# A planner's port model and durations: how a recording layer orders and places the instructions of a hybrid decoder layer

## The chip, the core and the metric

The kernel runs on one core of a Trainium2 chip. The metric is the device time of one execution in microseconds. Five engines work side by side, each through its own list of instructions in the order in which they were issued: TensorE (PE; its weight loads are shown as PEld), VectorE (DVE), ScalarE (ACT), GpSimd (POOL) and SyncE (SP, which here only starts DMAs). They wait for each other through semaphores. Matmuls write PSUM; the working memory is SBUF.

## What is computed

One layer of a hybrid decoder trunk in float32: 512 tokens of width 1024, 256 memory tokens, 4 heads in each of three groups, a feed-forward width of 2816. Cut to what matters:

```python
h = rmsnorm(x, norm_mix)
mem_h = rmsnorm(mem, norm_mem)
c_q, c_kv, k_rope, hq, hf, hi, hg, mq = split(h @ w_in)
y_mla = mla_group(c_q, c_kv, k_rope, ...)      # causal softmax attention, low-rank q and kv, rotary key
y_hg  = hgrn2_group(hq, hf, hi, hg, ...)       # gated linear recurrence
y_mem = mem_group(mq, mem_h, ...)              # softmax attention to 256 memory tokens
mix = concatenate([rmsnorm(y_mla), y_hg, rmsnorm(y_mem)])
x = x + mix @ w_out
h2 = rmsnorm(x, norm_ffn)
x = x + (silu(h2 @ w_gate) * (h2 @ w_up)) @ w_down
```

## The kernel before

**Products.** Every float32 operand of a large product is split into a high part, rounded to the matmul's type, and the rest: `split` makes `hi` on ACT (`A.copy`, or a scaled activation) and `lo = src - hi` on DVE, a `tensor_tensor` with two SBUF operands where the source is a weight. `mm3` then issues three matmuls for one product: hi x hi, hi x lo, lo x hi. In the trace the weights' parts are `wh` and `wl`, loaded into `wr` (or `mx` and `y` in the gate and up products); the activations' are `xh` and `xl`, `hd`, `v`, `mv`, `mx`, `pth` and `ptl`. PSUM tiles are `mm` (3 banks), `at` (3) and `tr` (2).

**Stages, in the order of the program:** x is split and its norm taken; HGRN2 with its levels (`hg_levels`, `hg_out`); the low-rank projections; rotary embedding (`rope`, on `qr` and `kr`) and causal attention by heads (`transposed`, `rope_t`, `softmax`, `weights_t`, `pv`), whose key transposes are `tr<-cst,tc`; attention to the memory; the output projection in two parts. The first part (blocks `OUT_ORDER[0:8]`) needs the first two groups and serves as filler beside the attention chains; the second (loop over `X_ORDER`) needs `group_norm` of the memory group: column sums, an inverse root in eleven small DVE instructions, four transposes `tr<-cst,sm` that spread it, then for each of four blocks a scaling on DVE, `xh` on ACT and `xl` on DVE. Behind each of the second part's eight blocks DVE adds the residual (`tm<-mm,tm`), scales (`y<-tm,RX`) and sums squares (`tc<-tc,tc`). Sums and differences of those blocks (tiles `p`, `td`) and their parts (`hd`, `v`, `mv`) are the left operands of the gate and up products: `fast` makes them by seven products instead of eight, in four rounds of columns (`FF`), with differences of weight blocks (`mx<-mx,mx`, `mx<-y,mx`) and of results. `down` (`mm` into `tr` or `mm`, `tr<-xh,wl` in the trace) is filled in between by `between`.

**What sets the order.** Nothing above is issued directly. `Recorder.record` (L102) takes down each call with its operands, its price (`price`, L183) and the other engines that can do the same (`others`, L160): an ACT copy can go to DVE; a DVE `tensor_tensor` on SBUF of at least 128 columns to POOL, with 500 ns added; a POOL `tensor_tensor` to DVE. `run` (L225) then plans: it keeps a time for each engine (`free`), for each instruction (`ready`, its predecessors' ends plus `LAT`) and for each buffer; again and again it takes, over all engines, the instruction that can start first, the more urgent one where two could start at once, and leaves an instruction to another engine where that would end it earlier. The result is one list in program order for each engine, and `issue` emits it. The engines on the chip keep each its own list's order, at their own speed. All instructions are thus issued from one line of the file, L350.

In the planner before, an engine is free when its own last instruction ends; what another engine does at that time doesn't matter. One price line of before, for POOL's `tensor_tensor`, and one for matmuls:

```python
return max(30 + 2.35 * m, 100 + 2.2 * m)
return (n * 0.417 + 3 if n >= 256 else 1.67 * n if n > 100 else 107) if ins[0].dtype == F32R else (1.676 * n if n > 100 else 214)
```

Of the kernel before, what the change touches and what calls it, by code (L numbers as in the profile page):

```python
# [20 lines left out]
NB = S // P  # L21
# [7 lines left out]
# columns of the packed vectors  # L29
# [16 lines left out]
class Recorder:  # L46
    """Takes down the instructions in program order, then issues them in an order
    that keeps the engines busy: by priority among those whose operands are there
    and whose buffers are free."""
# [20 lines left out]
    def last(self, eng):  # L70
        """the last instruction of an engine so far"""
        return next(o.n for o in reversed(self.ops) if o.eng == eng)

    @contextmanager
    def after(self, n):
        """keep back until an earlier instruction is through"""
        old, self.held = self.held, n
        yield
        self.held = old
# [22 lines left out]
    def record(self, eng, name, args, kw):  # L102
# [48 lines left out]
        o.alts = {eng: (name, args, kw, o.cost, 0)}  # L151
        for e, nm_, a, k in self.others(o, ins):
            q = _Op()
            q.eng, q.name, q.args, q.kw = e, nm_, a, k
            o.alts[e] = (nm_, a, k, self.price(q, outs, ins), {"gpsimd": 500}.get(e, self.MOVE if eng == "scalar" else 0))
# [4 lines left out]
    def others(self, o, ins):  # L160
        """other engines that do the same"""
# [20 lines left out]

    def price(self, o, outs, ins):  # L183
# [3 lines left out]
        if o.eng == "tensor":  # L187
            if o.name == "transpose":
                return 107
            if ins[0].dtype == F32 and self._free(ins[0]) <= 64 and n <= 64:  # L190
                return 65 if n <= 32 else 125
            return (n * 0.417 + 3 if n >= 256 else 1.67 * n if n > 100 else 107) if ins[0].dtype == F32R else (1.676 * n if n > 100 else 214)
        m = max([self._free(a) for a in ins] + [n])
        if o.eng == "scalar":
            fn = o.args[2] if o.name == "activation" else None
            if fn is not None:
                o.table = self.TABLES.get(str(fn).split(".")[-1])
            return 53 + 0.88 * m + (250 if "accum_out" in o.kw else 0) + (90 if hasattr(o.kw.get("scale"), "ap") else 0)
        if o.eng == "vector":
            if o.name == "reciprocal":  # L200
                return 70 + 6.6 * m
            fast = all(x.tensor.name not in self.tiles or self.tiles[x.tensor.name][4] == "SB" for x in ins)
# [13 lines left out]
        return max(30 + 2.35 * m, 100 + 2.2 * m)  # L216
# [8 lines left out]
    def run(self):  # L225
# [19 lines left out]
        table, dma, done, out = None, 0.0, 0, []  # L245
        busy = {e: 0.0 for e in engs}
        while done < len(ops):
            best = None
            for e in engs:
                be = None  # L250
                for o in cand[e]:
                    t = max(free[e], o.ready)
                    ok = True
# [20 lines left out]
                    if len(o.alts) > 1:  # L274
                        fin = t + o.alts[e][3] + o.alts[e][4]
                        late = False
                        for e2 in o.alts:
                            if e2 != e:
                                t2 = max(free[e2], o.ready)
                                if e2 == o.home or t2 + o.alts[e2][3] + o.alts[e2][4] < fin:  # L280
                                    back = sum(q.alts[e2][3] for q in cand[e2] if q.prio < o.prio and q.home == e2 and q.ready <= t2 + 200)
                                    if t2 + back + o.alts[e2][3] + o.alts[e2][4] < fin:
                                        late = True
# [15 lines left out]
            o.name, o.args, o.kw, cost, _ = o.alts[beste]  # L299
# [5 lines left out]
            end = t + cost  # L305
            free[o.eng] = end
# [67 lines left out]
def body(ctx, tc, t):  # L374
# [79 lines left out]
    def load(src, n=1024):  # L454
        """a [128, n] block of a weight"""
# [5 lines left out]
    def piece(raw, a, b):  # L461
        """some columns of a block, as their two parts"""
# [6 lines left out]
    def pieces(raw, n=1024):  # L469
        """k -> the k-th [128, 128] of a block, as its two parts"""  # L470
# [13 lines left out]
    def rsqrt_col(v, n):  # L484
        """v**-0.5 of a [128, n] block of positive numbers"""
# [9 lines left out]
    def colsum(sq, nblk):  # L495
        """column sums of [128, nblk*128], one per partition"""
# [5 lines left out]
    def spread(r):  # L502
        """[128, NB], by token, to [128, 512], the same on each partition"""
# [10 lines left out]
    def sumsq(srcs, acc=None, tag="td", eng=G):  # L514
        """elementwise sum of the squares of several [128, n] blocks"""
# [42 lines left out]
    def feat(dst, raw, acts):  # L558
        """dst [128 features, 512 tokens] from one block of columns"""
# [74 lines left out]
    def gated(i):  # L634
        """one block of the input projection, scaled by the norm of x"""
# [24 lines left out]
    def wide(src, n, banks, acts, use):  # L660
        """token-major products with one group of n columns"""
# [24 lines left out]
    def new_pt(ns):  # L686
        """transposed weights of two blocks of queries, keys on the partitions"""
        return sb("pth", (P, 8, P), F32R), sb("ptl", (P, 8, P), F32R)

    def pv(v, h, pt, ns, y):  # L690
        """y [128 values, 256 queries] of the products with ns blocks of keys"""
# [202 lines left out]
    # r * rsqrt(r^2 * mean + eps) by token and head  # L894
# [11 lines left out]
    def rope(src, nh):  # L906
        """rotate [128, NB, nh, 64] in place"""
# [51 lines left out]
    def transposed(src, h, scale=None):  # L959
        """one head of token-major blocks, by feature, as its two parts"""  # L960
# [8 lines left out]
    def softmax(src, nk, scale, neg, causal):  # L969
        """exp(scale * (src - max)) / sum by rows of a [128, nk] block of scores"""  # L970
# [12 lines left out]
    def weights_t(pp_, ns):  # L983
        """the softmax of two blocks of queries, transposed, as its two parts"""
# [8 lines left out]
    def group_norm(ys, i0, gname, tag):  # L993
        """RMS norm over four [128, 512] blocks, as operands of the output projection"""
# [8 lines left out]
    def rope_t(src, h):  # L1003
        """one head of [128, NB, 2, 64] blocks, by feature: their high parts and the source"""
# [115 lines left out]
    # a scale by token that keeps the tokens alike in size where sums of different ones are taken:  # L1120
    # about the norm so far; it goes out again with the norm
# [27 lines left out]
    # left operands of the seven products of the first layer, two blocks of inputs in each  # L1149
# [15 lines left out]
    def xsplit(src):  # L1165
        """two [128, 256] blocks, as the two parts"""
# [31 lines left out]
    def fast(src, c0, w, c):  # L1198
        """two groups of w columns, token-major, by the seven products of Winograd's form of
        Strassen's algorithm: over the halves of the tokens, of the inputs and of the columns"""  # L1200
# [63 lines left out]
    def between():  # L1264
        """a block of outputs of the second layer after every so many products"""
# [42 lines left out]
def pack(inp):  # L1308
    """the inputs as the program reads them: transposed and cut, values as they are"""
    c = np.ascontiguousarray  # L1310

    def kcut(w, cols):
        # [K, cols] -> [128, K/128 * cols]
# [73 lines left out]
```

## Time and profile before

| | us |
|---|---|
| device time, median of 3 runs | 799.17 (796.9 to 800.5) |
| span of the profiled execution, first to last instruction | 796.1 |
| mean granted TensorE clock in it | 0.980 |

The profile is of another execution than the three; only its span is known, and the median of the runs lies 3.1 us above it. A row of a group names the line, the engine, the operation, the tiles written and read (buffer numbers left out), the shape and the count; behind the bar the engine's busy time, the mean ns of one, then the idle time before these instructions and what ended it. A row of the timeline begins with the start in us from the span's start and the duration; in brackets stands the idle time before it and whose instruction ended it. Instructions of one engine overlap a little, so the step from one start to the next is shorter than a duration: a 128x384 instruction on DVE takes some 0.55 us and the next one starts 0.47 us after it.

### The profile page before, as it was taken

Reading aid. Unit: us, or ns where it says so; the run is one execution under the profiler, and the core shown is the slowest. Engines: PE = TensorE matmul, PEld = TensorE weight load, DVE = VectorE, ACT = ScalarE, POOL = GpSimd, SP = SyncE. Lnnn points to the kernel's source line nnn. Section 1 sums busy time; section 2 is a strip of 40 time slices with the busy share of each in tenths; the row PEclk is TensorE's granted clock in tenths of the full one; section 3 lists DMA queues with packets and bytes.
Section 4 is the critical chain, followed back from the end, with each engine's and each line's share of the span. In section 5 each row is a group of like instructions: output and inputs, shape, how many; then the busy total and the mean of one; then the engine's idle time right before and its main releaser. Section 6 shows DMA issues by size and latency. Waiting matters only on the chain. (4 is left out here: it accounts for less than half of the span.)

```text
span 796.1 us, 12214 instructions
## 1 busy us (share of the span) xinstructions
PE 742.4 (93%) x4117; PEld 646.8 (81%) x4117; DVE 620.7 (78%) x1267; ACT 382.3 (48%) x776; POOL 323.4 (41%) x324
## 2 busy tenths in 40 slices
PE   7999999997999998999959897989999899999998
PEld 4789877886788876888848796889988899989986
DVE  6977789848887789887899998666787768776572
ACT  7542325345665455654464653445444454545440
POOL 2434244326122335244784454443344433543331
PEclk9999999999899999899988999999999999999999
DMA  7221121104331322121512331242332423233132
GB/s 264 69 80 54 54 93 61 40 27 132 112 128 31 117 80 67 53 66 46 188 49 83 108 99 61 70 122 68 120 100 61 129 70 93 74 95 92 35 99 100
DMA packets 36207, 69.39 MB, mean 87 GB/s; under 512 B 4272, under 2 KB 21296, under 8 KB 36144
## 3 DMA queue, kind: packets, MB, share of 16 engines
q1 hardware_dynamic: 36144, 68.61, 27.1%
q8 instruction: 32, 0.52, 0.3%
q14 instruction: 31, 0.25, 0.1%
HBM read 66.50 MB, written 2.10 MB: 86 GB/s over the span
## 5 line engine op out<-in xcount | busy, mean ns | idle before, releaser
L350 ACT CAST wh<-wr 128x512 fp32r<-128x512 f32 (+2 forms) x149 | 85.0, 573 | 119.4 <-PE mm L350 67.9
L350 POOL TENSOR_TENSOR wl<-wr,wh 128x512 fp32r<-128x512 f32 (+2 forms) x54 | 68.7, 1274 | 139.5 <-PE mm L350 67.9
L350 ACT CAST wh<-mx 128x384 fp32r<-128x384 f32 (+1 forms) x158 | 76.3, 486 | 92.9 <-PE at L350 43.4
L350 PE MATMUL mm<-xh,wh 128*128 128x512 f32 x244 | 99.6, 410 | 10.2 <-ACT xh L350 5.6
L350 PE MATMUL mm<-xl,wh 128*128 128x512 f32 x244 | 99.9, 410 | 0.4 <-DVE xl L350 0.4
L350 PE MATMUL mm<-xh,wl 128*128 128x512 f32 x244 | 99.2, 407 | 0.0
L350 DVE TENSOR_TENSOR wl<-mx,wh 128x384 fp32r<-128x384 f32 (+1 forms) x128 | 82.5, 661 | 6.4 <-PE at L350 3.3
L350 DVE TENSOR_TENSOR wl<-wr,wh 128x512 fp32r<-128x512 f32 (+2 forms) x104 | 76.5, 745 | 12.3 <-ACT wh L350 3.8
L350 PE MATMUL mm<-wh,hd 128*128 128x384 f32 (+2 forms) x232 | 72.0, 335 | 0.8 <-DVE tm L350 0.8
L350 POOL TENSOR_TENSOR mx<-mx,mx 128x384 f32<-128x384 f32 (+1 forms) x42 | 49.9, 1193 | 46.1 <-DVE mx L350 26.4
L350 POOL TENSOR_TENSOR wl<-mx,wh 128x384 fp32r<-128x384 f32 (+1 forms) x32 | 31.6, 987 | 89.0 <-PE at L350 32.8
L350 DVE TENSOR_TENSOR tm<-tr,tm 128x512 f32<-128x512 f32 x30 | 20.7, 690 | 60.3 <-PE tr L350 60.3
L350 PEld LDWEIGHTS mm<-xh,wh 128*128 128x128 f32 x244 | 47.5, 195 | 20.4 <-ACT xh L350 6.9
L350 PE MATMUL tr<-xh,wl 128*128 128x512 f32 x132 | 52.8, 400 | 5.0 <-DVE wl L350 5.0
L350 PE MATMUL at<-wh,hd 128*128 128x384 f32 (+1 forms) x176 | 56.3, 324 | 0.0
L350 PEld LDWEIGHTS mm<-xl,wh 128*128 128x128 f32 x244 | 47.0, 192 | 10.7 <-DVE xl L350 2.4
L350 POOL TENSOR_TENSOR wl<-y,wh 128x384 fp32r<-128x384 f32 (+1 forms) x35 | 37.6, 1082 | 43.4 <-PE tr L350 18.1
L350 PEld LDWEIGHTS mm<-xh,wl 128*128 128x128 f32 x244 | 47.0, 192 | 7.4
L350 PE MATMUL tr<-xl,wh 128*128 128x512 f32 x132 | 52.2, 396 | 0.0
L350 PE MATMUL tr<-xh,wh 128*128 128x512 f32 x132 | 52.1, 395 | 0.0
L350 ACT CAST wh<-y 128x384 fp32r<-128x384 f32 (+1 forms) x63 | 30.3, 485 | 42.1 <-PE tr L350 20.8
L350 PEld LDWEIGHTS mm<-wh,hd 128*128 128x128 f32 x232 | 43.8, 193 | 3.0 <-ACT v L350 1.0
(384 smaller groups left out, 2081.0 us busy)
## 6 DMA issues: line engine op xcount, KB each, us to landing
wr<-in_wf SPq DMA_DIRECT2D x20, 512.0 KB, 3.3
wr<-in_wd SPq DMA_DIRECT2D x24, 384.0 KB, 3.1
mx<-in_wg SPq DMA_DIRECT2D x24, 192.0 KB, 2.6
y<-in_wg SPq DMA_DIRECT2D x24, 192.0 KB, 2.5
mx<-in_wu SPq DMA_DIRECT2D x24, 192.0 KB, 2.4
y<-in_wu SPq DMA_DIRECT2D x24, 192.0 KB, 2.5
tm<-in_xT SPq DMA_DIRECT2D x16, 256.0 KB, 3.6
wr<-in_wt SPq DMA_DIRECT2D x8, 512.0 KB, 3.7
```

The lines of the kernel that those rows point to most:

```text
L350: r = getattr(getattr(self.nc, o.eng), o.name)(*[get(a) for a in o.args], **{k: get(a) for k, a in o.kw.items()})
```

## The change

The planner's `run` gets a `port`: a time until which the SBUF port that DVE and POOL share is held. `shares` says which instructions hold it: POOL's `tensor_...` operations, and DVE's with two SBUF operands, or copies and scalings from SBUF to SBUF. Such an instruction is planned to start only when the port is free, and it keeps it to its end, on whichever engine it is placed. The prices are set anew: POOL's `tensor_tensor` at 170 + 2.17 ns a column (for 128x384 it was 945, and it is 1003), a 128x512 matmul 225.8 ns instead of 216.5, ACT by whether its source lies in SBUF. Comments and docstrings are dropped too, which changes nothing that is issued; L350 becomes L370.

```diff
-        o.alts = {eng: (name, args, kw, o.cost, 0)}
+        o.alts = {eng: (name, args, kw, o.cost, 0, self.shares(o, outs, ins))}
...
+    def inside(self, aps):
+
+        return all(x.tensor.name not in self.tiles or self.tiles[x.tensor.name][4] == "SB" for x in aps)
+
...
             if o.name == "transpose":
-                return 107
-            if ins[0].dtype == F32 and self._free(ins[0]) <= 64 and n <= 64:
-                return 65 if n <= 32 else 125
-            return (n * 0.417 + 3 if n >= 256 else 1.67 * n if n > 100 else 107) if ins[0].dtype == F32R else (1.676 * n if n > 100 else 214)
+                return 109
+            if ins[0].dtype == F32R:
+                return n / 2.4 + 12.5 if n >= 256 else max(1.67 * n, 107)
+            return 222 if n <= 2 else 62 if n <= 32 else 118 if n <= 64 else 218 if n <= 128 else 1.7 * n
...
-            return 53 + 0.88 * m + (250 if "accum_out" in o.kw else 0) + (90 if hasattr(o.kw.get("scale"), "ap") else 0)
+            return (92 if fast else 45) + 0.835 * m + (190 if "accum_out" in o.kw else 0) + (100 if hasattr(o.kw.get("scale"), "ap") else 0)
...
-        return max(30 + 2.35 * m, 100 + 2.2 * m)
+        return 170 + 2.17 * m
+
+    def shares(self, o, outs, ins):
+
+        if o.eng == "gpsimd":
+            return o.name.startswith("tensor")
+        if o.eng != "vector" or not self.inside(ins):
+            return False
+        if o.name in ("tensor_copy", "tensor_scalar"):
+            return self.inside(outs)
+        return o.name in ("tensor_tensor", "scalar_tensor_tensor") and sum(self._free(a) > 1 for a in ins) > 1
...
                     t = max(free[e], o.ready)
+                    if o.alts[e][5]:
+                        t = max(t, port)
...
                                 t2 = max(free[e2], o.ready)
+                                if o.alts[e2][5]:
+                                    t2 = max(t2, port)
...
             end = t + cost
+            if both:
+                port = end
```

What comes of it in the lists: POOL has 170 rows instead of 328, DVE 1413 instead of 1265, ACT 758 instead of 743; PE has the same matmuls in another order, and SP the same 253 rows. In the stretch from 380 to 490 us of the profile before, POOL's 51 instructions become 16 (41 go to DVE, 6 come from it); up to 180 us 83 become 64, from there to 380 us 68 become 35, and behind 490 us 118 become 47. Up to 380 us most matmuls of HGRN2 and of attention stand 12 to 81 places later among those of the projections; in the feed-forward part PE's order is nearly the same.

Three places in the lists. Rows are the operation, the tile written, the tiles read and the size; a tile's number names its buffer and is counted anew in each program.

*The start of attention, PE.* `tr<-cst,tc` are the transposes of the first head's rotary queries, `mm<-wh,hd` products of the keys' and values' projection, `mm<-wh,mx` those of the memory's. Before:

```order
L350 MATMUL mm_4105<-wh_3988,hd_3745 128x512
L350 MATMUL mm_4105<-wh_3996,hd_3810 128x512
L350 MATMUL mm_4105<-wl_4006,hd_3810 128x512
L350 MATMUL tr_4125<-cst,tc_4115 128x128 x4
L350 MATMUL mm_4105<-wh_3996,hd_3818 128x512
L350 MATMUL mm_4138<-wh_3988,hd_3735 128x512
```

With the change:

```order
L370 MATMUL mm_4131<-wl_4118,mx_3353 128x512
L370 MATMUL mm_4131<-wh_4092,mx_3384 128x512
L370 MATMUL mm_4139<-wh_4092,mx_3353 128x512
L370 MATMUL tr_4172<-cst,tc_4163 128x128 x4
L370 MATMUL mm_4139<-wl_4118,mx_3353 128x512
L370 MATMUL mm_4139<-wh_4092,mx_3384 128x512
```

The transposes moved from inside the last projection products to 23 places later, behind the rest of these and sixteen of the memory's.

*The memory norm and the second part of the output projection, PE and POOL.* On PE `tr<-cst,sm` spreads the norm, `mm<-mx,wh` are the last products of the first part, and `mm<-xh,wh` the first of a block that needs the norm's result. Before, the rows from the transposes on are these, then 48 more such `mm<-mx` and `mm<-xh` rows of the first part's blocks stand ahead of the second part:

```order
L350 MATMUL tr_6059<-cst,sm_6036 128x128 x4
L350 MATMUL mm_6009<-mx_5426,wh_5854 128x512
L350 MATMUL mm_6009<-mx_5411,wl_5947 128x512
L350 MATMUL mm_6009<-mx_5445,wh_5854 128x512
L350 MATMUL mm_6009<-mx_5456,wh_5854 128x512
L350 MATMUL mm_6009<-mx_5445,wl_5947 128x512
```

With the change:

```order
L370 MATMUL tr_6148<-cst,sm_6111 128x128 x4
L370 MATMUL mm_6086<-mx_5519,wl_6034 128x512
L370 MATMUL mm_6086<-mx_5547,wh_5948 128x512
L370 MATMUL mm_6086<-mx_5560,wh_5948 128x512
L370 MATMUL mm_6086<-mx_5547,wl_6034 128x512
L370 MATMUL mm_6178<-xh_6171,wh_6022 128x512
L370 MATMUL mm_6183<-xh_6171,wh_6057 128x512
L370 MATMUL mm_6187<-xh_6171,wh_6084 128x512
L370 MATMUL mm_6178<-xl_6198,wh_6022 128x512
```

Four matmuls are left between the transposes and the second part's first product, where there were 53. POOL's rows beside the second part's blocks, before:

```order
L350 TENSOR_TENSOR td_6273<-y_6301 128x256
L350 TENSOR_TENSOR hd_6275<-y_6301,hd_6265 128x256
L350 TENSOR_TENSOR hd_6353<-td_6273,hd_6343 128x512
L350 TENSOR_TENSOR p_6282<-y_6301,y_6341 128x256
L350 TENSOR_TENSOR v_6318<-y_6341,v_6292 128x256
L350 TENSOR_TENSOR p_6295<-p_6282,y_6301 128x256
L350 TENSOR_TENSOR hd_6391<-p_6282,hd_6379 128x512
L350 TENSOR_TENSOR hd_6409<-p_6295,hd_6401 128x512
L350 TENSOR_TENSOR hd_6430<-td_6306,hd_6420 128x512
```

With the change:

```order
L370 TENSOR_TENSOR td_6261<-y_6243 128x256
L370 TENSOR_TENSOR wl_6283<-wr_6189,wh_6247 128x512
L370 TENSOR_TENSOR wl_6312<-wr_6239,wh_6274 128x512
L370 TENSOR_TENSOR hd_6342<-y_6243,hd_6263 128x256
L370 TENSOR_TENSOR hd_6342<-y_6295,hd_6263 128x256
L370 TENSOR_TENSOR wl_6397<-mx_6162,wh_6368 128x384
L370 TENSOR_TENSOR wl_6430<-mx_6174,wh_6400 128x384
```

The sums, the differences and most of their parts went to DVE; two weights' rests of the last blocks and two of the first gate products stand on POOL in their place.

*The first gate round's results, POOL.* Beside DVE's `tc`, `td`, `tm` sums and the `wl<-wr,wh` that `down` needs, before:

```order
L350 TENSOR_TENSOR wl_7609<-mx_7137,wh_7598 128x384
L350 TENSOR_TENSOR mx_7576<-mx_7576,mx_7557 128x384
L350 TENSOR_TENSOR mx_7591<-mx_7591,mx_7581 128x384
L350 TENSOR_TENSOR wl_7656<-y_7151,wh_7639 128x384
L350 TENSOR_TENSOR mx_7626<-mx_7626,mx_7603 128x384
```

With the change:

```order
L370 TENSOR_TENSOR wl_7558<-mx_7112,wh_7550 128x384
L370 TENSOR_TENSOR wl_7609<-mx_7157,wh_7598 128x384
L370 TENSOR_TENSOR mx_7578<-mx_7578,mx_7571 128x384
L370 TENSOR_TENSOR wl_7787<-y_7215,wh_7755 128x384
L370 TENSOR_TENSOR wl_8053<-mx_7602,wh_8045 128x384
```

`wl_7609<-mx` is the same instruction in both pieces. Of the four rows behind it before, one `mx<-mx,mx` is still there; the two rows after that belong to later products. DVE's own rows there are the same seven in the same order.

More of the change, by code (lines that the diff above doesn't have):

```diff
@@ L154, in record @@
             q.eng, q.name, q.args, q.kw = e, nm_, a, k
-            o.alts[e] = (nm_, a, k, self.price(q, outs, ins), {"gpsimd": 500}.get(e, self.MOVE if eng == "scalar" else 0))
+            o.alts[e] = (nm_, a, k, self.price(q, outs, ins), {"gpsimd": 500}.get(e, self.MOVE if eng == "scalar" else 0), self.shares(q, outs, ins))
         self.ops.append(o)
@@ L188, in price @@
             if o.name == "transpose":
-                return 107
-            if ins[0].dtype == F32 and self._free(ins[0]) <= 64 and n <= 64:
-                return 65 if n <= 32 else 125
-            return (n * 0.417 + 3 if n >= 256 else 1.67 * n if n > 100 else 107) if ins[0].dtype == F32R else (1.676 * n if n > 100 else 214)
+                return 109
+            if ins[0].dtype == F32R:
+                return n / 2.4 + 12.5 if n >= 256 else max(1.67 * n, 107)
+            return 222 if n <= 2 else 62 if n <= 32 else 118 if n <= 64 else 218 if n <= 128 else 1.7 * n
         m = max([self._free(a) for a in ins] + [n])
+        fast = self.inside(ins)
         if o.eng == "scalar":
@@ L201, in price @@
                 return 70 + 6.6 * m
-            fast = all(x.tensor.name not in self.tiles or self.tiles[x.tensor.name][4] == "SB" for x in ins)
             if o.name == "tensor_copy":
@@ L244, in run @@
                     cand[e].append(o)
-        table, dma, done, out = None, 0.0, 0, []
+        table, dma, done, out, port = None, 0.0, 0, [], 0.0
         busy = {e: 0.0 for e in engs}
@@ L298, in run @@
             o.eng = beste
-            o.name, o.args, o.kw, cost, _ = o.alts[beste]
+            o.name, o.args, o.kw, cost, _, both = o.alts[beste]
             if o.eng != "scalar":
```

## The prediction

> **What bounds the kernel now.** First the page: the span, the busy times, the slices. TensorE (PE) is busy 93% of the span, and the granted clock (PEclk) sags in several slices.
>
> ```profile
> span 796.1 us, 12214 instructions
> PE 742.4 (93%) x4117; PEld 646.8 (81%) x4117; DVE 620.7 (78%) x1267; ACT 382.3 (48%) x776; POOL 323.4 (41%) x324
> PE   7999999997999998999959897989999899999998
> DVE  6977789848887789887899998666787768776572
> PEclk9999999999899999899988999999999999999999
> ```
>
> PE is idle 796.1 - 742.4 = 53.7 us, and that is all an order can give back, apart from the clock. The busy times by stage (projections and HGRN2; attention and first part of the output projection; its second part and the first gate and up products; the rest) say where the idle time lies. The columns are the stretch, its length, then PE, PEld, DVE, ACT and POOL busy, the granted clock and the DMA share with its rate.
>
> ```profile
> 0.00:180.00 180.00, 168.74 (x1040) 141.84 (x1041) 135.47 (x343) 75.55 (x143) 65.25 (x87) 1.00 0.25 83
> 180.00:380.00 200.00, 188.63 (x1009) 157.88 (x1008) 168.23 (x401) 111.34 (x232) 73.44 (x68) 0.97 0.25 84
> 380.00:490.00 110.00, 91.30 (x450) 80.93 (x449) 105.50 (x163) 57.37 (x114) 62.51 (x51) 0.94 0.33 103
> 490.00:796.00 306.00, 293.75 (x1624) 266.16 (x1622) 211.53 (x362) 138.03 (x288) 122.21 (x118) 0.99 0.29 86
> ```
>
> PE idles 11.3, 11.4, 18.7 and 12.3 us. In the third stretch VectorE (DVE) is busy 105.5 of 110 us: there DVE is the bound. Elsewhere PE is, with single stalls.
>
> Next the timeline, for why DVE is so slow there:
>
> ```profile
> 396.98 0.68 DVE L350 TENSOR_TENSOR wl<-wr,wh 128x512 fp32r<-128x512 f32 x1
> 397.02 1.24 POOL L350 TENSOR_TENSOR hd<-y,hd 128x256 fp32r<-128x256 f32 x1
> 397.58 1.22 DVE L350 TENSOR_TENSOR y<-tm,RX 128x512 f32<-128x512 f32 x1
> 398.31 1.64 POOL L350 TENSOR_TENSOR hd<-td,hd 128x512 fp32r<-128x512 f32 x1
> 398.73 1.78 DVE L350 TENSOR_TENSOR tc<-tc,tc 128x512 f32<-128x512 f32 x1
> ```
>
> The same size takes DVE 0.68, 1.22 or 1.78 us. The 1.78 one starts inside POOL's (GpSimd's) 1.64 and ends at 400.51, 0.56 after POOL's end at 399.95; the 1.22 one likewise ends 0.54 after POOL's end at 398.26. Two engines that read two SBUF operands take turns, whole instructions at a time; DVE's busy time holds the wait. With a PSUM operand there is none, which the groups of this stretch show:
>
> ```profile
> L350 DVE TENSOR_TENSOR wl<-mx,wh 128x384 fp32r<-128x384 f32 x39 | 28.1, 742 | 0.0
> L350 DVE TENSOR_TENSOR mx<-y,mx 128x384 f32<-128x384 f32 x15 | 11.7, 793 | 1.0 <-POOL mx L350 0.9
> L350 DVE TENSOR_TENSOR tc<-tc,tc 128x512 f32<-128x512 f32 x7 | 9.7, 1381 | 0.0
> L350 DVE TENSOR_TENSOR y<-tm,RX 128x512 f32<-128x512 f32 x8 | 7.9, 985 | 0.0
> L350 DVE TENSOR_TENSOR tm<-mm,tm 128x512 f32<-128x512 f32 x9 | 6.1, 680 | 3.0 <-PE mm L350 3.0
> L350 DVE TENSOR_TENSOR td<-mm,td 128x384 f32<-128x384 f32 x3 | 1.6, 546 | 0.0
> ```
>
> Against 546 and 680 ns the first four groups lose 39 x 0.20 + 15 x 0.25 + 7 x 0.70 + 8 x 0.31 = 18.9 us. Those are 70 instructions at 0.27 us each; some 40 more of this kind in smaller groups make, at the same rate, about 11 us (an estimate): **about 30 of DVE's 105.5 us are waits for the port**, 0.6 us for each of POOL's 51 instructions.
>
> **The change part by part.** The new table makes the planner hold back whichever engine would meet the other at the port. By the order, POOL's list falls from 328 to 170 rows and DVE's grows from 1265 to 1413. PE's work is the same; what can change is its waits and its clock. The new prices issue nothing of their own, and SyncE's list has the same 253 transfers in nearly the same order; both are costed at nothing: none of PE's stalls shown below ends with a transfer.
>
> *A, the stretch 380 to 490.* By the order 41 of POOL's 51 instructions here go to DVE and 6 come back; POOL keeps 16. On DVE they cost 18 x 0.47 (384 wide) + 8 x 0.60 (512 wide, the step from 396.98 to 397.58 above) + 15 x 0.33 (256 wide, scaled from these) = 18.2 us; the 6 that leave and a few casts that go to ScalarE (ACT) give back some 4.5. If each of the 16 still costs DVE 0.6 us of waiting, the waits fall from 30 to 10. Sum: +13.7 - 20 = -6.3 us. The bounds: -16 if the 16 cost nothing, +1 if each costs 1.05 (no wait seen is much longer than POOL's own instruction). Since DVE is the bound, PE gets this back, and with it half of the 3.0 us that the clock costs here (below): I take **-8**.
>
> The 0.47 comes from the feed-forward part, in the first rows here, which also carry the stall of *D*:
>
> ```profile
> 519.99 0.56 DVE L350 TENSOR_TENSOR tc<-at,tc 128x384 f32<-128x384 f32 x1
> 520.46 0.88 DVE L350 TENSOR_TENSOR td<-tm,td 128x384 f32<-128x384 f32 x1
> 520.89 2.62 POOL L350 TENSOR_TENSOR mx<-mx,mx 128x384 f32<-128x384 f32 x2
> 521.27 1.37 DVE L350 TENSOR_TENSOR tc<-tm,tc 128x384 f32<-128x384 f32 x1
> 522.56 2.65 DVE L350 TENSOR_TENSOR tm<-tm,tc 128x384 f32<-128x384 f32 x2
> 523.47 1.32 POOL L350 TENSOR_TENSOR wl<-y,wh 128x384 fp32r<-128x384 f32 x1
> 524.76 1.30 POOL L350 TENSOR_TENSOR mx<-mx,mx 128x384 f32<-128x384 f32 x1
> 525.13 1.81 DVE L350 TENSOR_TENSOR wl<-wr,wh 128x512 fp32r<-128x512 f32 x2
> 526.66 0.51 PE L350 MATMUL tr<-xh,wl 128*128 128x512 f32 x1 [2.09 <-DVE wl L350]
> ```
>
> *D, the feed-forward part.* Four DVE instructions before the `wl` that PE waits for meet four of POOL's and take about 1.3 us each instead of 0.47. In the new order DVE's rows up to that `wl` are the same, and of POOL's four one is left near. DVE comes through some 2.5 us earlier, and the 2.09 us stall goes. The fourth row of the next fence is its twin in the next round. With the clock behind the first, -5.9; I take **-5**.
>
> ```profile
> 198.78 1.11 PE L350 MATMUL tr<-cst,tc 128*128 128x128 f32 x4 [4.03 <-DVE tc L350]
> 316.60 0.79 PE L350 MATMUL mm<-xh,wh 128*128 128x512 f32 x1 [2.64 <-DVE xh L350]
> 416.33 1.87 PE L350 MATMUL tr<-ones,tc 128*128 128x2 f32 x8 [4.61 <-DVE tc L350]
> 628.07 0.51 PE L350 MATMUL tr<-xh,wl 128*128 128x512 f32 x1 [2.09 <-DVE wl L350]
> 628.41 0.40 PE L350 MATMUL tr<-xh,wh 128*128 128x512 f32 x1
> 628.64 0.40 PE L350 MATMUL tr<-xl,wh 128*128 128x512 f32 x1
> ```
>
> *B, the start of attention.* The transposes at 198.78 waited 4.03 us for a copy that stood in DVE's queue. They now stand 23 matmuls later (0.23 us each, the step of the last two rows: 5.3 us), and the copy goes to ACT. The stall is covered: -4.0.
>
> *C, the wait at 316.60.* Six POOL instructions around it go to DVE, which pays about 0.6 us for each and is spared a like wait. The order of the chain changes too, so I count a third of the stall and its clock: -2.
>
> The clock. After four of these stalls the granted clock is halved:
>
> ```profile
> 197.10:203.90 6.80, 5.12 (x14) 4.22 (x15) 5.67 (x19) 2.78 (x5) 1.17 (x3) 0.50 0.24 78
> 316.60:323.40 6.80, 6.39 (x16) 4.73 (x17) 5.76 (x12) 2.71 (x5) 1.28 (x1) 0.50 0.28 96
> 412.20:422.30 10.10, 5.97 (x21) 5.97 (x22) 10.10 (x13) 6.18 (x13) 6.96 (x7) 0.50 0.07 19
> 528.20:531.60 3.40, 3.40 (x10) 2.63 (x9) 0.15 (x1) 1.13 (x2) 1.00 (x1) 0.50 0.60 218
> 628.00:632.00 4.00, 3.94 (x17) 3.28 (x18) 1.75 (x5) 1.97 (x5) 1.01 (x1) 1.00 0.59 199
> ```
>
> Half of PE's busy time in each is lost: 2.6, 3.2, 3.0 and 1.7 us. B becomes **-6.6**; the others are counted in C, A and D. The Trainium skill, page "TensorE: Matmul & The Clock Gate", section "HAM oscillation", gives the rule that PE must not idle for more than about 3.4 us. By it only the 4.03 and the 4.61 us stall would cost clock, and the sum would be some 3 us smaller; the trace differs, since 2.64 and one of two stalls of 2.09 us are followed by 0.50.
>
> *N, new stalls.* The chains of HGRN2 and attention stand 12 to 81 matmuls later in PE's order, behind filler that then is used up. At the memory norm there were 53 matmuls between its transposes and the first product that needs its result; now there are 4. That product needs one DVE instruction of 0.6 us and one of ACT, and its second factor `xl` is DVE's eighth behind the transposes: 8 x 0.6 = 4.8 us, against 4 + 3 matmuls or 1.6 us of cover. That is a stall of **+3.3**, from 0 (filler elsewhere moves up) to 4.8. For what 148 more rows on DVE delay unseen I add +2.
>
> Sum: A -8, B -6.6, C -2, D -5, N +5.3 = -16.3: a span of 779.8 us. The three runs' median, 799.17, is 3.1 above this span, so the time is **783**.
>
> **The rivals.** *More of it (764).* If DVE is freed wholly in 380 to 490, PE's 18.7 us of idle there falls to about 5, and 3 us of clock come with it: A is -17. With B, all of C (-5.8) and D (-5.9), and no N: -35. For it: DVE's list in this stretch loses two thirds of its port partners. Against: the gates of the first round need DVE anyway.
>
> *Moved, not removed (797).* DVE's 105.5 us stay, because the moved work costs what the waits did (A 0), and B and D are made up by N at twice its size plus a halved clock behind it. For it: A's two halves are 13.7 and 20, not far apart. Against: the stalls of B and D have plain causes in the rows.
>
> *Slower (809).* The filler is gone before the chain's end. The memory norm's stall takes all the cover that it lost, 49 x 0.23 = 11.3 us, and 3.4 of halved clock; A begins that much later and gives nothing; only D's 5 us remain: +9.7. It decides from where `xl` stands over 40 matmuls (9 us) behind the transposes. Against: DVE's list has 8 instructions there, 4.8 us.
>
> **How the numbers follow.** The forecast has 0.5, more of it 0.17, moved 0.18, slower 0.15. The forecast's own range is 773 to 793, from A's bounds with N's. With 2 in 10 left out at both ends, the range is 767 to 802. A change of 0.5% (4 us) is about what a measurement of this kernel tells from none, so faster is below 795.2: 0.5 + 0.17 + 0.05 of the moved case = 0.72; the same 0.13; slower 0.15.
>
> **What would show it.** In the new profile POOL should be busy about 160 us and DVE no more than now. A: `tc<-tc,tc` at 0.7 to 0.9 us instead of 1.38, and PE idle under 12 us between the memory norm and the first feed-forward round's end. B and D: no wait over 1 us at the first key transposes and at the `tr<-xh,wl` products, and a clock of 1.00 there. N: a PE wait of some 3 us at the first `mm<-xh,wh` behind the memory norm. I am wrong if waits for DVE's `wl` grow instead, or if DVE's busy time rises by the 60 us and more that the moved instructions cost alone.

## The result, and the profile after

The changed kernel takes **767.58 us** (median of 4 runs, 766.0 to 769.33) against 798.03 us (median of 4, 794.35 to 800.5): a ratio of 0.9624, with a 95% interval of 0.9583 to 0.9665. The forecast was 783, with a range from 767 to 802, so the time lies 0.6 us inside the lower end of the range. The direction and most of the places were right; the gain is 30 us where 16 were forecast.

The span and the busy times of the changed kernel, as at the start of the prediction:

```profile
span 767.3 us, 12180 instructions
PE 734.7 (96%) x4117; PEld 646.9 (84%) x4117; DVE 615.1 (80%) x1415; ACT 391.6 (51%) x790; POOL 148.7 (19%) x166
```

POOL's busy time is more than halved, and DVE's does not rise although it has 148 more instructions. PE's idle time falls from 53.7 to 767.3 - 734.7 = 32.6 us, and its busy time by 7.7.

To see where, both spans are cut at the same places of the program: matmuls that stand at the same position in PE's list. The columns are the stretch, its length, then PE, PEld, DVE, ACT and POOL busy with their instructions, the granted clock, and the DMAs. Before:

```profile
0.00:184.70 184.70, 173.44 (x1080) 146.54 (x1081) 138.50 (x350) 77.90 (x148) 65.80 (x88) 1.00 0.25 86
184.70:204.00 19.30, 15.05 (x58) 11.75 (x57) 18.17 (x35) 11.15 (x22) 12.17 (x13) 0.82 0.26 84
204.00:312.00 108.00, 104.53 (x584) 87.90 (x583) 91.73 (x237) 64.46 (x134) 33.24 (x34) 1.00 0.27 92
312.00:340.00 28.00, 24.83 (x122) 20.22 (x121) 24.55 (x54) 14.03 (x31) 8.76 (x7) 0.88 0.20 64
340.00:380.40 40.40, 39.92 (x213) 33.64 (x212) 30.75 (x72) 19.36 (x43) 18.71 (x15) 1.00 0.20 65
380.40:487.40 107.00, 88.30 (x438) 78.01 (x437) 104.20 (x161) 55.75 (x112) 62.51 (x51) 0.95 0.34 105
487.40:639.60 152.20, 144.98 (x751) 132.17 (x750) 107.83 (x168) 71.38 (x141) 65.68 (x59) 0.98 0.30 90
639.60:796.10 156.50, 151.37 (x885) 136.59 (x883) 105.00 (x196) 68.27 (x151) 56.53 (x59) 0.99 0.27 81
```

With the change:

```profile
0.00:184.50 184.50, 174.77 (x1080) 150.05 (x1081) 136.70 (x370) 78.38 (x148) 46.31 (x69) 0.97 0.27 86
184.50:199.30 14.80, 13.46 (x59) 10.33 (x58) 14.62 (x21) 11.67 (x23) 12.70 (x11) 1.00 0.34 108
199.30:304.00 104.70, 104.70 (x580) 88.56 (x580) 91.49 (x259) 64.97 (x125) 13.74 (x17) 1.00 0.33 104
304.00:329.50 25.50, 23.52 (x122) 19.15 (x121) 22.52 (x59) 15.98 (x35) 1.28 (x1) 0.93 0.18 53
329.50:368.20 38.70, 37.70 (x216) 31.99 (x214) 29.54 (x81) 22.25 (x54) 5.36 (x7) 1.00 0.23 67
368.20:470.90 102.70, 89.54 (x438) 80.69 (x438) 97.37 (x194) 59.19 (x118) 19.75 (x16) 0.93 0.35 103
470.90:611.00 140.10, 139.99 (x752) 129.58 (x751) 113.33 (x207) 71.98 (x143) 28.10 (x26) 1.00 0.35 101
611.00:767.30 156.30, 151.03 (x884) 136.58 (x882) 109.50 (x231) 67.17 (x148) 21.46 (x22) 1.00 0.27 80
```

The lengths change by -0.2, -4.5, -3.3, -2.5, -1.7, -4.3, -12.1 and -0.2 us, together -28.8. Between 184 and 380 us the same position in the list doesn't mean the same work: with the change the third stretch has 319 products of 512 columns instead of 300 and the fifth 111 instead of 134, so some 2 to 3 us of work moved from the fifth to the third. The largest single part is the seventh stretch, the feed-forward part, where PE is now idle for 0.1 us and DVE has 39 more instructions for 5.5 us more. In the sixth, the DVE-bound one, DVE does 33 more instructions in 6.8 us less. Some of its groups with the change, as those of before in the prediction:

```profile
L370 DVE TENSOR_TENSOR wl<-mx,wh 128x384 fp32r<-128x384 f32 x37 | 20.6, 565 | 1.3 <-ACT wh L370 0.9 <-issue 0.2
...
L370 DVE TENSOR_TENSOR mx<-y,mx 128x384 f32<-128x384 f32 x16 | 8.6, 550 | 0.0
...
L370 DVE TENSOR_TENSOR y<-tm,RX 128x512 f32<-128x512 f32 x8 | 6.9, 865 | 0.2
L370 DVE TENSOR_TENSOR tm<-mm,tm 128x512 f32<-128x512 f32 x9 | 6.1, 680 | 0.0
L370 DVE TENSOR_TENSOR tc<-tc,tc 128x512 f32<-128x512 f32 x7 | 5.3, 758 | 0.0
```

Against 546 and 680 ns the four groups with two SBUF operands lose 0.7 + 0.1 + 1.5 + 0.5 = 2.8 us, where they lost 18.9.

The gain is not free of new waits. Four places in the timeline of the changed kernel: a product of HGRN2, the start of attention, the memory norm's first products, and the largest new stall:

```profile
132.47 0.38 PE L370 MATMUL at<-tm,tm 128*128 128x128 f32 x1 [1.88 <-POOL tm L370]
...
198.07 0.50 PE L370 MATMUL mm<-wh,mx 128*128 128x512 f32 x1 [1.34 <-DVE v L370]
...
368.17 0.98 PE L370 MATMUL mm<-xh,wh 128*128 128x512 f32 x3 [1.00 <-ACT xh L370]
...
370.11 3.29 DVE L370 TENSOR_TENSOR xl<-y,xh 128x512 fp32r<-128x512 f32 x4
371.65 0.54 PE L370 MATMUL mm<-xl,wh 128*128 128x512 f32 x1 [2.51 <-DVE xl L370]
...
427.37 0.69 PE L370 MATMUL mm<-wh,v 128*128 128x384 f32 x1 [5.38 <-ACT wh L370]
```

The waits at 368.17 and 371.65, 3.5 us, are the forecast's term N (3.3); the first, 1.0 us, ends the fifth stretch, the second lies in the sixth. The 5.38 us in the first gate round and the two at the top were not foreseen.

### The profile page after: what moved, and what is told of

Read it like the earlier page. It is cut to its first block, busy times and chain, and to the rows that moved or that the text cites. A ratio compares the mean times of both kernels' runs of the same rounds, so it can differ in the third digit from the quotient of the medians.

```text
span 767.3 us, 12180 instructions
## 1 busy us (share of the span) xinstructions
PE 734.7 (96%) x4117; PEld 646.9 (84%) x4117; DVE 615.1 (80%) x1415; ACT 391.6 (51%) x790; POOL 148.7 (19%) x166
## 4 chain that ended last, share of the span: by engine, by line
PE 64%; DVE 7%; issue 1%; DMA 1%; ACT 1%; DVEq 0%; ACTq 0%
PE mm L370 30%; PE tr L370 18%; PE at L370 17%; DVE wl L370 2%; DVE y L370 1%; DVE tm L370 1%; DVE p L370 1%; DMA mx<-in_wu 1%; DVE tc L370 1%; DVE mx L370 1%; DVE xl L370 0%; DVE hd L370 0%; DVE xh L370 0%; DVE sm L370 0%; DVE td L370 0%
## 5 line engine op out<-in xcount | busy, mean ns | idle before, releaser
L370 ACT CAST wh<-wr 128x512 fp32r<-128x512 f32 (+2 forms) x151 | 86.2, 575 | 120.6 <-PE mm L370 81.8
L370 ACT CAST wh<-mx 128x384 fp32r<-128x384 f32 (+1 forms) x160 | 77.5, 486 | 91.4 <-PE at L370 40.7
L370 PE MATMUL mm<-xh,wh 128*128 128x512 f32 x244 | 99.3, 410 | 7.1 <-ACT xh L370 7.1
L370 DVE TENSOR_TENSOR wl<-wr,wh 128x512 fp32r<-128x512 f32 (+2 forms) x141 | 96.7, 693 | 10.5 <-issue 4.0
L370 PE MATMUL mm<-xl,wh 128*128 128x512 f32 x244 | 99.4, 407 | 2.5 <-DVE xl L370 2.5
L370 PE MATMUL mm<-xh,wl 128*128 128x512 f32 x244 | 98.8, 405 | 0.0
L370 DVE TENSOR_TENSOR wl<-mx,wh 128x384 fp32r<-128x384 f32 (+1 forms) x141 | 74.1, 536 | 14.1 <-PE at L370 5.8
L370 PE MATMUL mm<-wh,hd 128*128 128x384 f32 (+2 forms) x232 | 71.2, 331 | 2.7 <-ACT wh L370 1.7
L370 PEld LDWEIGHTS mm<-xh,wh 128*128 128x128 f32 x244 | 46.9, 193 | 16.7 <-ACT xh L370 8.5
L370 PEld LDWEIGHTS mm<-xl,wh 128*128 128x128 f32 x244 | 46.9, 192 | 12.9 <-DVE xl L370 5.2
L370 PE MATMUL at<-wh,hd 128*128 128x384 f32 (+1 forms) x176 | 56.4, 325 | 0.0
L370 PEld LDWEIGHTS mm<-xh,wl 128*128 128x128 f32 x244 | 46.8, 192 | 8.6 <-DVE wl L370 0.4
L370 PE MATMUL tr<-xh,wl 128*128 128x512 f32 x132 | 52.0, 394 | 0.5 <-DVE wl L370 0.5
L370 PE MATMUL tr<-xl,wh 128*128 128x512 f32 x132 | 51.9, 393 | 0.0
L370 PE MATMUL tr<-xh,wh 128*128 128x512 f32 x132 | 51.7, 392 | 0.0
L370 ACT CAST wh<-y 128x384 fp32r<-128x384 f32 (+1 forms) x64 | 30.9, 486 | 35.4 <-PE at L370 19.5
L370 PE MATMUL mm<-wh,v 128*128 128x384 f32 (+1 forms) x128 | 42.5, 336 | 5.9 <-ACT wh L370 5.4
L370 PEld LDWEIGHTS mm<-wh,hd 128*128 128x128 f32 x232 | 43.0, 189 | 5.5 <-ACT wh L370 2.0
L370 DVE TENSOR_TENSOR tm<-tr,tm 128x512 f32<-128x512 f32 x30 | 20.6, 687 | 31.9 <-PE tr L370 31.9
L370 POOL TENSOR_TENSOR wl<-mx,wh 128x384 fp32r<-128x384 f32 (+1 forms) x19 | 19.3, 1016 | 129.4 <-PE at L370 51.6
L370 PE MATMUL at<-wh,v 128*128 128x384 f32 (+1 forms) x128 | 41.8, 330 | 0.0
L370 POOL TENSOR_TENSOR wl<-wr,wh 128x512 fp32r<-128x512 f32 (+2 forms) x17 | 21.4, 1264 | 104.6 <-PE mm L370 55.6
```

The costliest lines, as they stand in the source:

```text
L370: r = getattr(getattr(self.nc, o.eng), o.name)(*[get(a) for a in o.args], **{k: get(a) for k, a in o.kw.items()})
```

## The experiments

The theory: the gain comes of the port, that is of POOL's sums and differences that DVE no longer meets. Rivals: the new prices make the better order; or it is only which engine does the work; or only the order that keeps the engines apart; or a lucky order.

**1 and 2: one half of the change each.** Run 1 has the new prices and leaves the port out:

```diff
-            if both:
-                port = end
```

> The changed planner with its new prices, but the port is never held (the two lines that set it are left out). By the order its lists are again like those of before: 325 rows on POOL and 1272 on DVE, against 328 and 1265 before and 170 and 1413 with the change. Theory (the port model makes the gain, because it takes instructions off POOL): 790 to 802 us, as before, and tc<-tc,tc again above 1.2 us. Rival (the realistic prices make a better order, the port does little): 765 to 778 us.

Run 2 has the port and puts the function `price` of the kernel before in place of the new one.

> The port model with the prices of before. POOL has 184 rows, DVE 1402. Theory (port): most of the gain, 766 to 778 us. Rival (prices): 790 to 802 us. If both are needed together, both of these runs stay above 782.

Run 1 took 807.69 us, 1.0104 of before (1.0063 to 1.0144): 1% longer, where the theory gave 790 to 802. Run 2 took 768.48, ratio 0.9613 (0.9583 to 0.9643), as the whole change. By themselves the prices lose 1%, and beside the port they change nothing that can be measured.

**3 to 5: the engine or the order.** A table fixes the engine of each instruction, and the planner only orders the lists (run 3: engines of after, planner of before; run 4: engines of before, changed planner; run 5: as run 4 with the prices of before):

```diff
         for o in ops:
+            e = {"T": "tensor", "V": "vector", "A": "scalar", "G": "gpsimd", "S": "sync"}[PLACE[o.n]]
+            o.home, o.alts = e, {e: o.alts[e]}
             o.left = len(o.preds)
```

> Each instruction is put on the engine on which the changed kernel has it (171 rows on POOL), by a table; the order of each list is then planned by the planner of before, which knows no port and has the old prices. If what counts is which engine does the work (fewer POOL instructions, fewer waits): 766 to 776 us. If what counts is the order, so that the two engines don't meet: 785 to 800 us. In between, both count.

> The reverse: each instruction on the engine on which the kernel before has it (328 rows on POOL), and the order planned by the changed planner, with port and new prices. If the engine counts: 790 to 805 us, with POOL busy above 300 us. If the order counts: 768 to 780 us.

> As the run with the engines of before and the order of the changed planner, but with the prices of before, so that the port alone is new in the order: 328 rows on POOL. If the port's order helps by itself once the new prices are out of it: 775 to 788 us. If the order and the engines only pay together: 792 to 803 us. DVE should be busy some 20 us less than before's 620.7 in either case, since the order keeps the two engines apart.

Run 3 took 789.81 us (0.988, 0.985 to 0.9909), run 4 801.85 (1.0034, 1.0011 to 1.0057) and run 5 800.18 (1.0008, 0.9988 to 1.0028). By the ranges set beforehand run 3 spoke for the order and run 4 for the engines, so by itself neither half does it: the engines alone give about 10 us of 30, the order alone nothing. Yet in run 5 the order did what it is for. Its busy times:

```profile
PE 744.3 (93%) x4117; PEld 653.7 (82%) x4117; DVE 595.4 (75%) x1267; ACT 384.0 (48%) x778; POOL 311.9 (39%) x324
```

DVE has the same 1267 instructions as before and needs 595.4 us for them, not 620.7: 25 us of waits are gone, and the time is the same (the table behind the last run shows where it went).

**6 and 7: the price of one sum on POOL.** In the changed kernel, 56 instructions more on POOL in the first gate and up round, outside the plan, so that the other lists stay as they are (run 7 has two `G.memset(junk[:, 0:600], 0.0)` at the same place):

```diff
+                if c0 == 0:
+                    rec.extra = True
+                    with rec.after(rec.last("tensor")):
+                        G.tensor_tensor(junk[:, 0:384], RX[:, 0:384], RX[:, 128:512], ALU.add)
+                    rec.extra = False
```

> The changed kernel with 56 more instructions on POOL in the first gate and up round (sums of 128x384 from SBUF into a tile that is no longer used, one behind each group of matmuls), which the planner doesn't count; every other list is as in the changed kernel. If a POOL sum costs DVE 0.6 us of waiting, as the prediction took: DVE busy 25 to 40 us more, and 15 to 30 us more in time, since DVE is nearly always busy there. If the two engines hardly meet, under 10 us of DVE and under 5 us of time. At the upper bound of the prediction, 1.05 us each: 59 us of DVE.

> The same 56 places, each with two fills of 600 columns on POOL, which write SBUF for about as long as a sum takes but read nothing. If it is the reading port that the engines share: DVE busy as in the changed kernel within 4 us, time within 4 us of it (what is left is that POOL's own work stands behind the fills). If any SBUF work of POOL's holds DVE up: like the run with the sums.

They took 808.19 and 787.48 us. The busy times of run 6, 52 of its 56 extra sums (between 400 and 520 us) and a group of DVE's beside them (between 400 and 500):

```profile
PE 745.6 (92%) x4117; PEld 655.5 (81%) x4117; DVE 653.3 (81%) x1415; ACT 392.0 (49%) x790; POOL 214.8 (27%) x222
...
L376 POOL TENSOR_TENSOR qr<-RX 128x384 f32<-128x384 f32 x52 | 62.3, 1199 | 3.6
...
L376 DVE TENSOR_TENSOR wl<-mx,wh 128x384 fp32r<-128x384 f32 x34 | 28.0, 831 | 0.7 <-PE at L376 0.4 <-issue 0.2
```

The same of run 7, and a row of its timeline:

```profile
PE 734.8 (93%) x4117; PEld 648.0 (82%) x4117; DVE 614.5 (78%) x1415; ACT 392.2 (50%) x790; POOL 214.7 (27%) x278
...
L376 POOL MEMSET qr<- 128x600 f32 x104 | 62.3, 599 | 5.7
...
L376 DVE TENSOR_TENSOR wl<-mx,wh 128x384 fp32r<-128x384 f32 x36 | 19.7, 553 | 12.5 <-PE at L376 12.4
...
492.18 0.69 PE L376 MATMUL mm<-wl,v 128*128 128x384 f32 x1 [9.87 <-POOL wl L376]
```

The sums cost DVE 653.3 - 615.1 = 38.2 us, **0.68 us each**; the fills, with POOL busy just as long, cost it nothing (614.5). It is reading that the two engines share. The Trainium skill, page "SBUF — State Buffer", section "Who interferes with whom", says so: a DVE instruction with two SBUF inputs contends with a GpSimd instruction that reads SBUF, not with one that only writes it. By that rule the fills are free for DVE, and the runs agree. In time, though, the fills cost 19.9 us, where under 4 were expected: up to 18 of them stand in a row in POOL's list ahead of a `wl` of POOL's own, and PE waits 7.99 and 9.87 us for two `wl` behind such rows. So the 40.6 us of run 6, where 15 to 30 were expected, can't all be put down to the port; its DVE time can.

**8: the new stall.** The ten small DVE instructions of the feed-forward norm, which stand ahead of what PE waits for at 427.37, are kept back:

```diff
-    V.tensor_tensor(r2, rms(x1s, D), lv, ALU.mult)
+    v2 = small(NB)
+    V.tensor_scalar(v2, colsum(x1s, NB), 1.0 / D, EPS, ALU.mult, ALU.add)
+    marks = []
...
+        if c0 == 0:
+            with rec.after(marks[3]):
+                V.tensor_tensor(r2, rsqrt_col(v2, NB), lv, ALU.mult)
```

> The changed kernel, with the ten small DVE instructions of the inverse root for the feed-forward norm kept back until the third product of the first gate round is through (its result is only read behind the round's last product). They stand in DVE's list ahead of the weight difference for which PE waits 5.38 us at 427.37, the largest stall that the change made. If they cause it: the stall falls under 2.5 us, its half-clock stretch of 6.8 us goes, and the time is 760 to 765 us. If the weights' sums would be late anyway: 766 to 769 us, with the stall at 4 us or more.

It took 766.4 us (0.9601, 0.9568 to 0.9634), the same as the changed kernel within the intervals. In its timeline the stall is a little smaller and still there:

```profile
425.30 0.45 PE L370 MATMUL mm<-wh,v 128*128 128x384 f32 x1 [4.19 <-ACT wh L370]
```

The theory that this chain causes the stall fell, by the 4 us that had been named for it. In the changed kernel DVE is busy 97.4 of 102.7 us in this stretch, so what stands in its list may be late there in any order; that is not shown, and the cause of the stall stays open.

**9 and 10: how far does a plan move by chance?** One number that has nothing to do with the port, `MOVE = 775`, set to 700, in the kernel before (run 9) and in the changed one (run 10).

> The kernel before with one number of its planner changed that has nothing to do with the port: what is added when ACT's work is offered to DVE, 700 ns instead of 775. It shows how far a plan without the port moves by chance. If the two single halves of the change stand 10 to 16 us behind the kernel before up to the feed-forward part because they are worse: 792 to 804 us here, with that part as in the kernel before within 5 us. If the order before was a lucky one there: 802 to 815 us, the loss up to the feed-forward part.

> The changed kernel with the same number at 700 instead of 775. If the gain is the port model's: 762 to 774 us. If half of it is a lucky order up to the feed-forward part: 774 to 786 us.

They took 792.63 us (0.9926, 0.9895 to 0.9958) and 763.1 us (0.9561, 0.9534 to 0.9588). The number moves either kernel by under 1%, and both the same way; the 30 us between them stay.

**11 and 12: no sums on POOL at all.** In the changed planner (run 11) and in the planner of before, with old prices and no port (run 12):

```diff
+        if eng == "gpsimd" and name == "tensor_tensor":
+            eng = "vector"
...
-                return [("gpsimd", "tensor_tensor", a, k)]
+                return []
```

> The changed planner, and POOL gets no sums or differences at all (34 rows, 1540 on DVE); six scalings and the fills stay. By the runs with extra work a sum of POOL's costs DVE 0.68 us of waiting where both are busy, and DVE does it alone in 0.47 (384 wide): DVE busy stays within 10 us of the changed kernel's 615 and the time at 762 to 772 us. If POOL's remaining 130 do real work because the planner puts them where DVE does not meet them: DVE busy 40 us and more up, and 775 to 795 us.

> The kernel before, without port and with its old prices, and one rule: POOL gets no sums or differences (45 rows on POOL, 1531 on DVE). If the port model pays because it takes POOL's sums away: 760 to 772 us, like the run of the changed planner with the same rule (764.34). If the port model or the new prices do more than that: 775 us and more.

Run 11 took 764.34 us (0.9581, 0.9552 to 0.9609): POOL's remaining help is worth nothing. Its busy times:

```profile
PE 734.3 (96%) x4117; PEld 648.6 (85%) x4117; DVE 634.5 (83%) x1540; ACT 396.7 (52%) x802; POOL 6.3 (1%) x29
```

POOL has 137 instructions fewer than in the changed kernel, and DVE is busy 19.4 us more: nearly twice the 10 that were expected at most, but only 0.14 us for each that POOL lost. But run 12, with the same rule, took 788.81 (0.989, 0.9866 to 0.9914), where 760 to 772 was expected.

**Where the runs differ.** All spans cut at one place, the transposes `tr<-cst,p` behind the first gate and up round. PE's idle time is the length less PE's busy time:

| run | sums on POOL | port | prices | first part | PE idle, clock in it | second part |
|---|---|---|---|---|---|---|
| before | many | no | old | 486.7 | 41.3, 0.98 | 309.4 |
| 9, other number | many | no | old | 484.8 | 40.7, 0.98 | 310.0 |
| 1 | many | no | new | 496.0 | 48.2, 0.97 | 309.7 |
| 5 | as before | order only | old | 496.5 | 44.8, 0.95 | 299.7 |
| 4 | as before | order only | new | 499.1 | 43.5, 0.95 | 299.0 |
| 3 | as after | engines only | old | 491.7 | 40.6, 0.95 | 296.2 |
| 12 | none | no | old | 490.4 | 39.1, 0.95 | 295.4 |
| 2 | few | yes | old | 471.1 | 30.2, 0.97 | 295.0 |
| after | few | yes | new | 470.7 | 27.2, 0.97 | 296.6 |
| 10, other number | few | yes | new | 465.6 | 26.4, 0.98 | 296.6 |
| 11 | none | yes | new | 466.9 | 23.8, 0.97 | 295.2 |

Two of the rows behind it, both parts of before and of run 12, with columns as above:

```profile
0.00:486.70 486.70, 445.37 (x2480) 377.43 (x2481) 407.20 (x903) 242.56 (x485) 201.20 (x206) 0.98 0.27 88
486.70:796.10 309.40, 297.05 (x1637) 269.39 (x1637) 213.53 (x365) 139.72 (x291) 122.21 (x118) 0.99 0.28 86
```

```profile
0.00:490.40 490.40, 451.29 (x2484) 389.85 (x2484) 403.02 (x1043) 256.46 (x509) 16.04 (x40) 0.95 0.28 87
490.40:785.80 295.40, 290.61 (x1635) 266.54 (x1633) 235.12 (x489) 139.94 (x292) 0.00 (x0) 1.00 0.31 90
```

*The second part* is settled. It takes 309 to 310 us in the three plans that let POOL's sums meet DVE, 299 to 300 where they are as many but kept apart, and 295 to 297 where they are few or none, whatever the prices. POOL's 118 instructions there spared DVE 235.1 - 213.5 = 21.6 us, 0.18 each, and took POOL 122 us.

*The first part* is not. Fewer sums or the port's order alone leave it 4 to 12 us longer than before, so DVE's waits are not what binds it by themselves; only the port with few sums (runs 2, 10, after), or the new prices with none (run 11; without sums the port has next to nothing left to hold), bring it to 466 to 471. In runs 3 and 12 PE idles 39 to 41 us there, in those four 24 to 30, and the clock is 0.95 against 0.97 and 0.98. PE's longest sum of waits up to 386 us in run 12:

```profile
PE at L352 <- DVE tm L352: 7.3, 5, 1.8
```

These are steps of HGRN2's chain that no filler covers any more. Run 3 loses its time elsewhere: the same wait is 0.9 us there, PE has done 1662 matmuls in its first 300 us against 1661 before, and the loss comes behind them, with a clock of 0.90 from 300 to 400 us against 0.97. So the two plans do not share that cause. Why the old prices without the port lead to such orders, or whether this is chance in two plans, stays open; the planner of before with the new prices and no sums on POOL was not run. A number without meaning for the port moved the first part by 1.9 and 5.1 us, not by 20 (the profile of run 9 is of its longest execution, 3.9 us above its median), but the prices are a larger change than that one number.

## Why the prediction was right, and where it was not

*A, the stretch 380 to 490, with N.* Right in mechanism, and nearly in size. The stretch fell by 4.3 us with 2.5 of N's 3.5 us of new stall in it: -6.8 for A alone, against -8. PE's idle time without N's fell by 8.0 us, but the 1.5 us that the clock was to give back did not come: it is 0.93 there instead of 0.95, and PE is busy 1.2 us longer. DVE's busy time there fell by 6.8, against 6.3 (the two terms of that sum, moved work and waits, were not measured apart); `tc<-tc,tc` takes 758 ns, in the 0.7 to 0.9 that was named. The 0.6 us that a POOL instruction costs DVE were measured as 0.68. PE idles 102.70 - 89.54 = 13.2 us there, just over the 12 that were named; 5.38 of them are the stall that the forecast did not have.

*B, the start of attention.* Right, and over-sized: -4.5 against -6.6. The 4.03 us stall and the half clock are gone (the clock is 1.00), but a wait of 1.34 us for `v` stands close behind, at 198.07. PE's idle time fell by 2.9 us and its busy time by 1.6, where 4.0 and 2.6 were put.

*C.* -2.5 against -2.

*D, the feed-forward part.* Right in mechanism, and the term that was most mis-sized: -12.3 (the last two stretches) against -5. The forecast priced the two stalls of 2.09 us and one stretch of half clock. The view of waits of PE behind 487.4 us, before:

```profile
PE tr L350 <- DVE wl L350: 5.0, 3, 2.1
PE tr L350 <- DVE xl L350: 1.8, 3, 0.9
```

and behind 470.9 us, with the change:

```profile
PE tr L370 <- DVE p L370: 0.5, 1, 0.5
PE tr L370 <- DVE xl L370: 0.5, 1, 0.5
PE tr L370 <- DVE wl L370: 0.5, 1, 0.5
```

Nearly all of DVE's lateness went, not that of two places: PE's idle time in the two stretches fell by 7.0 us, where 4.2 were in the two stalls, and its busy time by 5.3. With it went a second half-clock stretch, behind the last stall of A in the profile of before, which was in no term of the sum:

```profile
486.70 0.41 PE L350 MATMUL tr<-cst,p 128*128 128x128 f32 x2 [2.87 <-DVE p L350]
...
487.20:490.60 3.40, 3.40 (x15) 3.33 (x14) 1.69 (x3) 1.82 (x4) 0.34 (x1) 0.50 0.02 5
```

At half speed those 3.4 us of PE cost 1.7, as much as the stretch that was in the sum; what the rest of the 5.3 us is stays open. The step "DVE comes through some 2.5 us earlier" was worked out for one place; that it holds throughout this part, runs 3, 5, 11 and 12 show by its length.

*The unseen +2.* Wrong in sign, and with D the term that failed most: the three stretches that had no term of their own lost 0.2, 3.3 and 1.7 us, and 2.7 instead of 1.7 without the 1.0 us of N that lies in the last of them. Between 199.3 and 304.0 us PE has no idle time left, where it had 3.5. The later chains did not run out of filler, except at the memory norm and for the 1.88 us at 132.47.

*Prices at nothing.* Right beside the port (run 2 against the change), wrong alone (run 1, +1%). With no sums on POOL, prices and port together make 24 us (runs 11 and 12), though the port has little left to hold there; which of the two does it was not tried.

The terms add up: A with N +1.4, B +2.1, C -0.5, D -7.3 and the unseen -8.2 make the span 12.5 us shorter than forecast, and the runs' median lies 0.3 us above the profiled span, not 3.1. That the time still fell inside the range was narrow, and owed to the range's width more than to the sum. The rival "more of it" gave 764, near the time, but by A's place (-17), which is not where the time went.

Part of the half clock only moved: with the change it also stands behind the wait of 1.88 us at 132.47, where before there was none. The stretch in the columns of the windows:

```profile
133.00:139.90 6.90, 6.25 (x24) 5.46 (x23) 5.36 (x20) 1.20 (x3) 1.51 (x2) 0.51 0.04 15
```

By the rule that the prediction cited from the Trainium skill, "TensorE: Matmul & The Clock Gate", section "HAM oscillation", that wait is too short to cost clock; the trace differs here as before.

## What to carry to other kernels

Before work is moved to a helper engine that shares a port, compare what the busy engine is spared with what it pays: here 118 instructions on POOL spared DVE 0.18 us each and cost POOL 1 us each, and the changed planner's plan without any of them was as fast as its plan with the few that it chose. Busy time that falls in a profile is not a gain by itself: 25 us less of it on DVE gave nothing, since the first part of that plan lost what the second gained. Parts of a plan (engines, order, prices) were worth 1.2%, nothing and -1% alone, and the port model that sets engines and order together 3.9%, so each is to be measured alone and together, and against a plan moved by a number without meaning.

## What was not expected of the hardware

The clock was halved in the changed kernel without an idle stretch before it. Columns as above, and the timeline of PE ahead of it:

```profile
168.00:170.60 2.60, 2.60 (x20) 2.47 (x21) 2.17 (x11) 0.80 (x2) 0.00 (x0) 1.00 0.24 96
170.60:174.00 3.40, 3.40 (x9) 2.65 (x9) 1.01 (x7) 0.82 (x2) 0.00 (x0) 0.50 0.00 0
```

```profile
167.89 1.05 PE L370 MATMUL mm<-ones,td 128*128 128x2 f32 x8 [0.21 <-DVE td L370]
...
169.58 0.95 PE L370 MATMUL tr<-ones,td 128*128 128x2 f32 x8
```

PE's only wait there is 0.21 us, and else it is shown busy; 16 of its matmuls in those 3 us are only 2 columns wide. Runs 8 and 10 show the same: 16 such matmuls and 0.2 us of waiting from 169.7 and from 163.1 us on, and half the clock 3.4 us later. In the kernel before 16 of them stand between 169.8 and 173.2 us with PE busy 3.39 of 3.40 us, and the clock stays at 1.00. This would fit if such products counted in part as idle for the clock; no run varies them alone. On the other hand the 1.34 us wait at 198.07 was followed by a full clock.

The traces also suggest why one of the two stalls of 2.09 us before was followed by half the clock and its twin was not. In one profile the stretches of half clock begin whole multiples of 3.413 us apart (before: at 197.09, 316.56, 412.13, 487.22 and 528.18 us, which is 35, 28, 22 and 12 steps). The step that holds the first stall, and the two that share its twin:

```profile
524.80:528.20 3.40, 1.53 (x7) 1.27 (x8) 3.40 (x6) 2.05 (x4) 1.26 (x1) 1.00 0.11 16
623.80:627.20 3.40, 2.17 (x12) 1.74 (x11) 3.40 (x4) 1.35 (x4) 3.40 (x3) 1.00 0.09 34
627.20:630.60 3.40, 2.54 (x11) 2.11 (x12) 2.55 (x5) 2.22 (x6) 0.26 (x1) 1.00 0.35 108
```

PE is idle 1.9 us in the first, and half the clock follows; in the other two it is idle 1.2 and 0.9, and none does. What seems to count is the idle time within one such step, not the length of a stall: in this profile and that of the changed kernel, behind the first 30 us, 1.7 us and more at full clock was followed by half of it, and 1.6 and less was not, but for the 16 small matmuls. The limit is not sharp: in run 5, 1.91 us from 123.9 us on was not.
